# Layer norm's two halves on ScalarE and VectorE, the second token tile's transposes three steps earlier, and the first w1 pieces split by GpSimd

## The chip, the cores and the metric

The kernel runs on one core of one Trainium2 chip. The metric is the device time of one execution in microseconds; a verdict rests on the median of several runs.

## What is computed

Two transformer layers over 512 tokens of width 1024, in float32. Layer 0 mixes tokens with a top-k attention over a compressed key, layer 1 with a differential attention; each is followed by a squared-ReLU MLP of width 4096. What bears on the change is the frame around them:

```python
for i in range(DEPTH):
    sh_t, sc_t, g_t, sh_c, sc_c, g_c = jnp.split(mod[i], 6, axis=-1)
    h = x * (1.0 + sc_t) + sh_t
    y = mixer_i(h)
    x = _layer_norm(DN_ALPHA * x + (1.0 + g_t) * y, ln_g[i, 0], ln_b[i, 0])
    h = x * (1.0 + sc_c) + sh_c
    y = jnp.square(jax.nn.relu(h @ w1)) @ w2
    x = _layer_norm(DN_ALPHA * x + (1.0 + g_c) * y, ln_g[i, 1], ln_b[i, 1])
```

So there are four layer norms: after each mixer, after the first MLP, and at the end of the kernel.

## The kernel before

The 512 tokens are four tiles of 128 rows (i = 0 to 3). The residual `R[i]` is two pages of 128x512 floats, the halves h = 0 and 1 of the 1024 features. Every matrix product is made of three fp32r matmuls: an operand is split into a high part and a low part (`split_sb`, L131: ScalarE casts the high part, VectorE or GpSimd subtracts it), and `mm3` (L156 to L160) multiplies low by high, high by high and high by low. A weight piece is loaded and split by `wpiece` (L138 to L154): ScalarE casts 128x1024 at L148, then L153 subtracts, in one instruction on VectorE or in two of 128x512 on GpSimd; without an engine named, the pieces take turns.

The end of a mixer is `mixer_out.rest` (from L1005). For each tile and half the output projection takes 24 matmuls (eight steps k of three, L984 to L986) into one PSUM bank, called (i, h) here. `add_scaled` (L485) multiplies the bank by the gain on VectorE (L488) and adds the product to `R[i][h]` on VectorE or GpSimd (L489). Then `finish` (L537) makes the layer norm: `bn_stats` of both halves (L494), `bn_aggr` (L496), 1/sqrt(variance + eps) in two GpSimd instructions (L386, L387), and both halves normalised by VectorE (L549). `to_hT` (L518) transposes the tile on TensorE, four 128x128 blocks a half into a bank of the tag `t` (L522; these eight matmuls are called T0 to T3 by tile), applies scale and shift of the next stage, either on ScalarE in four 128x128 pieces (L533) or on VectorE in two 128x512 instructions (L527, L529), and splits the result into `hth` and `htl` (L133, L134). There are two banks `t` and three buffers `bm` for the result of scale and shift.

Behind it the MLP begins. Its first four w1 pieces (n = 0 to 3) run over tokens 0 to 255 first, 24 matmuls of 128x256 each, so that they need only tiles 0 and 1; then the same pieces run over tokens 256 to 511, for which tiles 2 and 3 must be in `hth` and `htl`.

A tile scheduler sets the order of the instructions on each engine. It goes by its own estimate of times and by constraints that the source gives: the table handed to `mixer_out` says behind which transposes a step of the projection may be issued, `{(2, 1, 3): "lead", (3, 1, 0): 0, (3, 1, 3): 1}` meaning that step k = 0 of (3, 1) comes behind T0 and k = 3 of (3, 1) behind T1. Once built, an engine runs its list strictly in that order, and DMAs are issued by SP in its order.

Of the kernel before, what the change touches and what calls it, by code (L numbers as in the profile page):

```python
# [15 lines left out]
ALU = mybir.AluOpType  # L16
# [51 lines left out]
def hybrid_kernel(  # L68
# [36 lines left out]
    def small(shape, tag, bufs=4):  # L105
        return tp.tile(shape, F32, tag=tag, name=nm(tag), bufs=bufs)
# [277 lines left out]
    def rstd_of(var, scale, tag):  # L384
        r = small([P, 1], tag)
        nc.gpsimd.tensor_scalar(out=r, in0=var, scalar1=scale, scalar2=EPS, op0=ALU.mult, op1=ALU.add)  # L386
        nc.gpsimd.tensor_tensor(out=r, in0=r, in1=mhalf, op=ALU.pow)  # L387
        return r
# [82 lines left out]
    def gain(l, v, tag="pg"):  # L471

        g1 = small([P, 8], "g1", 2)
        nc.vector.tensor_scalar(out=g1, in0=modc[:, l, v, :], scalar1=1.0, scalar2=None, op0=ALU.add)
        g = [temp(tag) if tag in TB else page(tag=tag) for _ in range(2)]
        for h in range(2):
            o = bank("t")
            for m in range(4):
                nc.tensor.matmul(o[:, P * m : P * (m + 1)], g1[:, 4 * h + m : 4 * h + m + 1].to_broadcast([P, P]), ident,
                                 start=True, stop=True)  # L480
            nc.scalar.copy(g[h], o)
        return g


    def add_scaled(R, h, o, g, eng):  # L485
# [2 lines left out]
        nc.vector.tensor_tensor(out=t, in0=o, in1=g[h], op=ALU.mult)  # L488
        eng.tensor_tensor(out=R[h], in0=R[h], in1=t, op=ALU.add)  # L489

    def ln_stats(R):
        st = small([P, 2, 6], "bnst")
        for h in range(2):
            nc.vector.bn_stats(out=st[:, h, :], in_=R[h])  # L494
        mv = small([P, 2], "bnmv")
        nc.vector.bn_aggr(out=mv, in_=st)  # L496
        return mv, rstd_of(mv[:, 1:2], 1.0, "lnr")

    def ln_pages(l, s, tag):
        res = []  # L500
# [17 lines left out]
    def to_hT(R, i, A, B, hT):  # L518
        for h in range(2):
            tb = bank("t")  # L520
            for m in range(4):
                last = nc.tensor.transpose(tb[:, P * m : P * (m + 1)], R[h][:, P * m : P * (m + 1)], ident)  # L522
            v = temp("bm")
            vv = v.rearrange("p (m t) -> p m t", m=4)
            if (h+i)%2:
                c = slice(4 * h, 4 * h + 4)
                nc.vector.tensor_tensor(out=vv, in0=tb.rearrange("p (m t) -> p m t", m=4),  # L527
                                        in1=A[:, c].unsqueeze(2).to_broadcast([P, 4, P]), op=ALU.mult)
                nc.vector.tensor_tensor(out=vv, in0=vv, in1=B[:, c].unsqueeze(2).to_broadcast([P, 4, P]), op=ALU.add)  # L529
            else:  # L530
                for m in range(4):
                    k = 4 * h + m
                    nc.scalar.activation(v[:, P * m : P * (m + 1)], tb[:, P * m : P * (m + 1)], AF.Identity,  # L533
                                         scale=A[:, k : k + 1], bias=B[:, k : k + 1])
            split_sb(vv, hT[0][:, 4 * h : 4 * h + 4, P * i : P * (i + 1)], hT[1][:, 4 * h : 4 * h + 4, P * i : P * (i + 1)],
                     nc.vector)
        return last.ins  # L537

    def finish(R, i, ln, coef, hT):
        mv, r = ln_stats(R)  # L540
        if coef is None:
            for h in range(2):
                nc.vector.scalar_tensor_tensor(out=R[h], in0=R[h], scalar=mv[:, 0:1], in1=ln[0][h], op0=ALU.subtract,
                                               op1=ALU.mult)
                nc.vector.scalar_tensor_tensor(out=R[h], in0=R[h], scalar=r, in1=ln[1][h], op0=ALU.mult, op1=ALU.add)
                nc.sync.dma_start(out[P * i : P * (i + 1), 512 * h : 512 * (h + 1)], R[h])
            return
        for h in range(2):
            nc.vector.tensor_scalar(out=R[h], in0=R[h], scalar1=mv[:, 0:1], scalar2=r, op0=ALU.subtract, op1=ALU.mult)  # L549
        later.append((R, ln))  # L550
        return to_hT(R, i, coef[0], coef[1], hT)

# [15 lines left out]
    def out_proj(w, act, nk, lead, tags, engs):  # L568
# [20 lines left out]
        R, g, fin = yield  # L589
        for i, o in zip(lead, os):  # L590
            add_scaled(R[i], 0, o, g, nc.gpsimd)
        for i in range(NT):
            if i not in lead:
                o = wide_bank()
                for k in range(nk):
                    step(pcs, o, i, k)
                add_scaled(R[i], 0, o, g, nc.gpsimd)
        pcs = pieces(1)
        if fin is None:
            os = [wide_bank() for i in range(NT)]  # L600
            for k in range(nk):
                for i in range(NT):
                    step(pcs, os[i], i, k)
            for i in range(NT):
                add_scaled(R[i], 1, os[i], g, nc.gpsimd)
        else:
            for i in range(NT):
                o = wide_bank()
                for k in range(nk):
                    step(pcs, o, i, k)  # L610
                add_scaled(R[i], 1, o, g, nc.vector)
                if i > 0:
                    fin(i - 1)
            fin(NT - 1)
# [347 lines left out]
    def mixer_out(w, src, R, ln_idx, prepare, mT, ring, order, late=lambda: None):  # L962
# [46 lines left out]
        def rest():  # L1009
            late()  # L1010
            mT.extend(new_hT())
            tags = {(1, 1): "l", (2, 0): "l", (2, 1): "o", (3, 0): "d", (3, 1): "d"}
            for i in range(NT):
                for h in range(2):
                    if (i, h) not in acc:
                        acc[i, h] = bank(tags[i, h])
                        for k in range(8):
                            m = [marks[order[t]] for t in order if t <= (i, h, k)]
                            with tc.issue_after(m[-1]) if m else nullcontext():
                                step(i, h, k)  # L1020
                    add_scaled(R[i], h, acc[i, h], gc[0], nc.vector if i in (0,) or (i, h) == (3, 1) else nc.gpsimd)
                marks[i] = finish(R[i], i, ln_idx, gc[1], mT)

        return weights(), first, rest
# [20 lines left out]
            for h in range(2):  # L1045
                nc.scalar.activation(R[i][h], R[i][h], AF.Copy, scale=ALPHA)

    attend(range(8), make_a, work, pv_a, done_a, mixer_out(a_w_o[0], oA, R, (0, 0), before_out_a, mT, 6, {(2, 1, 3): "lead", (3, 1, 0): 0, (3, 1, 3): 1}, scale_residual), 4, topk, 2, 2, side)


    def mlp(l, hT, ln_idx, coef_fn, side):
# [4 lines left out]
        for q in range(4):  # L1056
# [22 lines left out]
            ws, os = [], []  # L1079
            for n in range(8):  # L1080
                c0 = 1024 * q + P * n
                w = wpiece((8, P), w1[:, :, c0 : c0 + P])
                o = wide_bank()
                if q == 0 and n < 4:
                    ws.append(w)
# [8 lines left out]
                    act(o)  # L1094
            if q == 0:
                for _ in range(3 if l == 0 else 0):
                    next(side, None)
                gc = gain(l, 5, "vo")
            fin = None
            if q == 3:  # L1100
# [107 lines left out]
    def done_b(p):  # L1208
# [15 lines left out]
        for i in range(NT):  # L1224
# [4 lines left out]

    mT = []  # L1230
    attend(range(8), make_b, None, pv_b, done_b,
           mixer_out(b_w_o[0], oB, R, (1, 0), lambda: (gain(1, 2, "hk"), next_coeffs(1, 0, 1, 3, 4)), mT, 6, {(2, 1, 3): "lead", (3, 1, 0): 0, (3, 1, 3): 1}), 3,
           tick=affine_later())
    mlp(1, mT, (1, 1), None, iter(()))

# [29 lines left out]
```

## Time and profile before

| | us |
|---|---|
| median of three runs | 1312.59 (1311.4 to 1314.78) |
| the profiled execution's own time | 1311.5 |
| its span | 1309.7 |
| TensorE busy in the span | 1267.0 (97%) |
| VectorE, ScalarE, GpSimd busy | 741.5, 504.2, 570.5 |

The span is what the profiler sees of the execution; 1.8 us of its own time lie around it. Times inside the span count from its start. "Granted clock" is the share of TensorE's full clock that it was given in a stretch: 1.00 is 2.4 GHz, 0.50 is 1.2 GHz.

### The profile page before, as it was taken

The numbers are of one execution on the slowest core, as the hardware profiler recorded it, in microseconds if no ns is written. First come the engines' busy times: TensorE is split into PE (matmuls) and PEld (weight loads), VectorE is DVE, ScalarE is ACT, GpSimd is POOL, SyncE is SP. The second block draws the span as 40 slices with busy tenths as digits, with TensorE's granted clock in tenths as the row PEclk, the third lists the DMA queues.
The fourth block names the chain that finished last, engine by engine and source line by source line (L and its number), as shares of the span: only waits on it lengthen the run. The fifth ranks groups of instructions, "written<-read, shape, count | busy, mean of one in ns | idle before, by whom it ended". The sixth has DMA issues, their size and how long they took to land.

```text
span 1309.7 us, 17697 instructions
## 1 busy us (share of the span) xinstructions
PE 1267.0 (97%) x6354; PEld 1013.4 (77%) x6354; DVE 741.5 (57%) x1553; ACT 504.2 (38%) x965; POOL 570.5 (44%) x469
## 2 busy tenths in 40 slices
PE   6999999998999999999999999999899999999997
PEld 4775566677988878878788898877798888888885
DVE  2487859968642774764646376684853342332437
ACT  2554247824432422412315555682453232231320
POOL 1614348604486235234134873451539623424403
PEclk9999999999999999999999999999999999999998
DMA  9727577543623684684422633440144333333311
GB/s 308 215 82 223 168 199 200 150 137 104 187 93 108 201 256 118 210 277 141 141 81 65 177 82 104 129 129 1 49 145 125 100 97 97 97 97 97 97 49 64
DMA packets 169135, 176.79 MB, mean 135 GB/s; under 512 B 13564, under 2 KB 121432, under 8 KB 169048
## 3 DMA queue, kind: packets, MB, share of 16 engines
q1 hardware_dynamic: 169048, 175.67, 45.1%
q8 instruction: 50, 0.82, 0.3%
q14 instruction: 37, 0.30, 0.1%
HBM read 160.93 MB, written 2.12 MB: 124 GB/s over the span
## 4 chain that ended last, share of the span: by engine, by line
PE 72%; DVE 6%; POOL 2%; issue 1%; ACT 1%; DMA 0%; POOLq 0%; DVEq 0%
PE psd L158 5%; PE psd L160 5%; PE psd L159 5%; PE psl L158 3%; PE psl L159 3%; PE psl L160 3%; PE psl L578 3%; PE psl L580 3%; PE psl L579 3%; PE pso L580 3%; PE pso L578 3%; PE psd L580 3%; PE pso L579 3%; PE pso L158 3%; PE psd L578 3%; PE pso L159 3%
## 5 line engine op out<-in xcount | busy, mean ns | idle before, releaser
L153 POOL TENSOR_TENSOR wl<-raw,wh 128x512 fp32r<-128x512 f32 (+1 forms) x226 | 302.2, 1361 | 505.5 <-ACT wh L148 477.7
L148 ACT CAST wh<-raw 128x1024 fp32r<-128x1024 f32 x181 | 189.8, 1050 | 425.0 <-PE psd L580 77.9
L153 DVE TENSOR_TENSOR wl<-raw,wh 128x1024 fp32r<-128x1024 f32 x68 | 91.1, 1339 | 150.0 <-ACT wh L148 150.0
L158 PE MATMUL psd<-htl,wh 128*128 128x512 f32 (+1 forms) x400 | 157.0, 392 | 3.2 <-DVE htl L134 2.7
L159 PE MATMUL psd<-hth,wh 128*128 128x512 f32 (+1 forms) x400 | 155.1, 388 | 0.0
L160 PE MATMUL psd<-hth,wl 128*128 128x512 f32 (+1 forms) x400 | 154.7, 387 | 0.0
L489 POOL TENSOR_TENSOR rq<-rq,pt 128x512 f32<-128x512 f32 x66 | 96.7, 1495 | 76.2 <-DVE pt L488 76.1
L158 PEld LDWEIGHTS psd<-htl,wh 128*128 128x128 f32 x400 | 76.6, 191 | 25.9 <-DVE htl L134 6.0
L679 ACT ACTIVATE ex<-neg,mx 128x128 f32<-128x128 f32 (+3 forms) x128 | 72.1, 564 | 50.3 <-DVE mx L673 42.5
L160 PEld LDWEIGHTS psd<-hth,wl 128*128 128x128 f32 x400 | 76.7, 192 | 16.3 <-issue 1.7
L159 PEld LDWEIGHTS psd<-hth,wh 128*128 128x128 f32 x400 | 76.7, 192 | 13.7 <-issue 0.8
L158 PE MATMUL psl<-htl,wh 128*128 128x512 f32 (+1 forms) x224 | 82.2, 367 | 4.2 <-DVE htl L134 4.2
L159 PE MATMUL psl<-hth,wh 128*128 128x512 f32 (+1 forms) x224 | 81.9, 366 | 0.0
L160 PE MATMUL psl<-hth,wl 128*128 128x512 f32 (+1 forms) x224 | 81.3, 364 | 0.0
L134 DVE TENSOR_TENSOR pg<-ex,pg 128x512 fp32r<-128x512 f32 x66 | 60.4, 917 | 27.1 <-ACT pg L133 27.1
L580 PE MATMUL psl<-wh,pg 128*128 128x512 f32 x176 | 68.9, 391 | 0.0
L578 PE MATMUL pso<-wh,pg 128*128 128x512 f32 x176 | 68.8, 391 | 0.0
L580 PE MATMUL pso<-wh,pg 128*128 128x512 f32 x176 | 68.7, 390 | 0.0
L578 PE MATMUL psl<-wh,pg 128*128 128x512 f32 x176 | 68.7, 390 | 0.0
L579 PE MATMUL pso<-wl,pg 128*128 128x512 f32 x176 | 68.7, 390 | 0.0
L579 PE MATMUL psl<-wl,pg 128*128 128x512 f32 x176 | 68.5, 389 | 0.0
L159 PE MATMUL pso<-hth,wh 128*128 128x512 f32 (+2 forms) x184 | 68.3, 371 | 0.0
(311 smaller groups left out, 2920.9 us busy)
## 6 DMA issues: line engine op xcount, KB each, us to landing
raw<-in_mlp_w_dram SPq DMA_DIRECT2D x128, 512.0 KB, 4.1
raw<-in_ada_w_dram SPq DMA_DIRECT2D x32, 512.0 KB, 4.2
hk<-in_ada_w_dram SPq DMA_DIRECT2D x48, 256.0 KB, 3.6
bm<-in_ada_w_dram SPq DMA_DIRECT2D x48, 256.0 KB, 4.9
raw<-in_b_w_in_dram SPq DMA_DIRECT2D x24, 512.0 KB, 4.0
pg<-pg SPq DMA_DIRECT2D x84, 128.0 KB, 2.4
pg<-in_ada_w_dram SPq DMA_DIRECT2D x32, 256.0 KB, 6.0
raw<-in_a_w_in_dram SPq DMA_DIRECT2D x14, 512.0 KB, 5.1
```

The costliest lines, as they stand in the source:

```text
L134: eng.tensor_tensor(out=L, in0=src, in1=f(H), op=ALU.subtract)
L148: nc.scalar.copy(Hv, r)
L153: eng.tensor_tensor(out=Lv[:, a:b], in0=r[:, a:b], in1=f(Hv[:, a:b]), op=ALU.subtract)
L158: nc.tensor.matmul(o, w[0], a[1], start=first, stop=False)
L159: nc.tensor.matmul(o, w[0], a[0], start=False, stop=False)
L160: nc.tensor.matmul(o, w[1], a[0], start=False, stop=last)
L489: eng.tensor_tensor(out=R[h], in0=R[h], in1=t, op=ALU.add)
L578: nc.tensor.matmul(o, al[1], wr[0], start=(k == 0), stop=False)
L579: nc.tensor.matmul(o, al[0], wr[1], start=False, stop=False)
L580: nc.tensor.matmul(o, al[0], wr[0], start=False, stop=(k == nk - 1))
L679: marks["a"] = nc.scalar.activation(e[:, 0:W], neg[:, 0:W], AF.Exp, bias=mx[:, 0:1], scale=-1.0, accum_out=sums[:, m : m + 1]).ins
```

## The change

The statistics of a half are taken as soon as it is summed (`half_stats`). The variance gets its eps on VectorE, and GpSimd keeps only the power. Half 0 is normalised on ScalarE, by scale and bias (the bias, minus mean times 1/std, is one more small VectorE instruction), half 1 on VectorE as before. The result of scale and shift goes to buffers of the tag `ex`, of which there are six, where it went to the three of `bm`; VectorE's share of it is now four instructions of 128x128 with two scalars where it was two of 128x512. The sums of tile 1 move from GpSimd to VectorE. In the table, T0 now stands ahead of step 5 of (3, 0) and T1 ahead of step 0 of (3, 1). The first four w1 pieces of an MLP are all split by GpSimd. The gain's broadcast is written as a transpose.

```diff
             for m in range(4):
-                nc.tensor.matmul(o[:, P * m : P * (m + 1)], g1[:, 4 * h + m : 4 * h + m + 1].to_broadcast([P, P]), ident,
-                                 start=True, stop=True)
+                nc.tensor.transpose(o[:, P * m : P * (m + 1)], g1[:, 4 * h + m : 4 * h + m + 1].to_broadcast([P, P]), ident)
...
+    halves = {}
+
+    def half_stats(R, h):
+
+        if id(R) not in halves:
+            halves[id(R)] = small([P, 2, 6], "bnst")
+        nc.vector.bn_stats(out=halves[id(R)][:, h, :], in_=R[h])
+
     def ln_stats(R):
-        st = small([P, 2, 6], "bnst")
-        for h in range(2):
-            nc.vector.bn_stats(out=st[:, h, :], in_=R[h])
         mv = small([P, 2], "bnmv")
-        nc.vector.bn_aggr(out=mv, in_=st)
-        return mv, rstd_of(mv[:, 1:2], 1.0, "lnr")
+        nc.vector.bn_aggr(out=mv, in_=halves.pop(id(R)))
+        v = small([P, 1], "bnve")
+        nc.vector.tensor_scalar(out=v, in0=mv[:, 1:2], scalar1=EPS, scalar2=None, op0=ALU.add)
+        r = small([P, 1], "lnr")
+        nc.gpsimd.tensor_tensor(out=r, in0=v, in1=mhalf, op=ALU.pow)
+        return mv, r
...
-            v = temp("bm")
+            v = temp("ex")
             vv = v.rearrange("p (m t) -> p m t", m=4)
             if (h+i)%2:
-                c = slice(4 * h, 4 * h + 4)
-                nc.vector.tensor_tensor(out=vv, in0=tb.rearrange("p (m t) -> p m t", m=4),
-                                        in1=A[:, c].unsqueeze(2).to_broadcast([P, 4, P]), op=ALU.mult)
-                nc.vector.tensor_tensor(out=vv, in0=vv, in1=B[:, c].unsqueeze(2).to_broadcast([P, 4, P]), op=ALU.add)
+                for m in range(4):
+                    k = 4 * h + m
+                    nc.vector.tensor_scalar(out=v[:, P * m : P * (m + 1)], in0=tb[:, P * m : P * (m + 1)],
+                                            scalar1=A[:, k : k + 1], scalar2=B[:, k : k + 1], op0=ALU.mult, op1=ALU.add)
...
-        for h in range(2):
-            nc.vector.tensor_scalar(out=R[h], in0=R[h], scalar1=mv[:, 0:1], scalar2=r, op0=ALU.subtract, op1=ALU.mult)
+        nm = small([P, 1], "lnm")
+        nc.vector.tensor_scalar(out=nm, in0=mv[:, 0:1], scalar1=r, scalar2=-1.0, op0=ALU.mult, op1=ALU.mult)
+        nc.scalar.activation(R[0], R[0], AF.Identity, scale=r, bias=nm)
+        nc.vector.tensor_scalar(out=R[1], in0=R[1], scalar1=mv[:, 0:1], scalar2=r, op0=ALU.subtract, op1=ALU.mult)
...
-                    add_scaled(R[i], h, acc[i, h], gc[0], nc.vector if i in (0,) or (i, h) == (3, 1) else nc.gpsimd)
+                    add_scaled(R[i], h, acc[i, h], gc[0], nc.vector if i < 2 or (i, h) == (3, 1) else nc.gpsimd)
+                    half_stats(R[i], h)
                 marks[i] = finish(R[i], i, ln_idx, gc[1], mT)
...
-{(2, 1, 3): "lead", (3, 1, 0): 0, (3, 1, 3): 1}
+{(2, 1, 3): "lead", (3, 0, 5): 0, (3, 1, 0): 1}
...
-                w = wpiece((8, P), w1[:, :, c0 : c0 + P])
+                w = wpiece((8, P), w1[:, :, c0 : c0 + P], nc.gpsimd if q == 0 and n < 4 else None)
```

How the built order moves, at the three places of the first mixer's end that count (the second mixer's end is alike). On TensorE around T0: `psd_3591` and `psd_3606` are the bank (3, 0), `psd_3619` is (3, 1), `rq_3001` and `rq_3003` are the halves of tile 0. Before:

```order
L984 MATMUL psd_3591<-pg_2738,vo_3380 128x512
L985 MATMUL psd_3591<-pg_2740,pg_3379 128x512
L986 MATMUL psd_3591<-pg_2738,pg_3379 128x512
L522 MATMUL pst_3418<-ident,rq_3001 128x128 x4
L522 MATMUL pst_3430<-ident,rq_3003 128x128 x4
L984 MATMUL psd_3619<-wh_1953,vo_3041 128x512
L985 MATMUL psd_3619<-wl_1954,pg_3040 128x512
```

Now:

```order
L992 MATMUL psd_3606<-wh_2393,vo_3174 128x512
L993 MATMUL psd_3606<-wl_2394,pg_3173 128x512
L994 MATMUL psd_3606<-wh_2393,pg_3173 128x512
L530 MATMUL pst_3421<-ident,rq_3001 128x128 x4
L530 MATMUL pst_3433<-ident,rq_3003 128x128 x4
L992 MATMUL psd_3606<-wh_2515,vo_3219 128x512
L993 MATMUL psd_3606<-wl_2516,pg_3218 128x512
```

T0 stood behind all 24 matmuls of (3, 0) and stands behind 15 of them; T1 moved from 9 matmuls into (3, 1) to its start, and T2 from 15 matmuls behind T1 to 24 behind it.

On VectorE between the first `bn_aggr` and the normalisation of tiles 0 and 1 (`bnmv_3411` is tile 0, `bnmv_3474` and `bnmv_3479` are tile 1, `bnmv_3562` and `bnmv_3572` are tile 2). Before:

```order
L496 BN_AGGR bnmv_3411<-bnst_3408 128x2
L488 TENSOR_TENSOR pt_3556<-pso_3531,hk_3020 128x512
L494 BN_STATS bnst_3559<-rq_3009 128x6
L496 BN_AGGR bnmv_3474<-bnst_3471 128x2
L549 TENSOR_SCALAR rq_3001<-rq_3001,bnmv_3411,lnr_3413 128x512
L549 TENSOR_SCALAR rq_3003<-rq_3003,bnmv_3411,lnr_3413 128x512
L494 BN_STATS bnst_3559<-rq_3011 128x6
L549 TENSOR_SCALAR rq_3005<-rq_3005,bnmv_3474,lnr_3476 128x512
L549 TENSOR_SCALAR rq_3007<-rq_3007,bnmv_3474,lnr_3476 128x512
L496 BN_AGGR bnmv_3562<-bnst_3559 128x2
L488 TENSOR_TENSOR pt_3616<-psd_3591,hk_3019 128x512
L549 TENSOR_SCALAR rq_3009<-rq_3009,bnmv_3562,lnr_3564 128x512
```

Now:

```order
L500 BN_AGGR bnmv_3411<-bnst_3405 128x2
L496 BN_STATS bnst_3541<-rq_3009 128x6
L496 BN_STATS bnst_3448<-rq_3007 128x6
L502 TENSOR_SCALAR bnve_3413<-bnmv_3411 128x1
L500 BN_AGGR bnmv_3479<-bnst_3448 128x2
L496 BN_STATS bnst_3541<-rq_3011 128x6
L502 TENSOR_SCALAR bnve_3481<-bnmv_3479 128x1
L557 TENSOR_SCALAR lnm_3417<-bnmv_3411,lnr_3415 128x1
L559 TENSOR_SCALAR rq_3003<-rq_3003,bnmv_3411,lnr_3415 128x512
L500 BN_AGGR bnmv_3572<-bnst_3541 128x2
L557 TENSOR_SCALAR lnm_3485<-bnmv_3479,lnr_3483 128x1
L559 TENSOR_SCALAR rq_3007<-rq_3007,bnmv_3479,lnr_3483 128x512
```

The last statistic of tile 2 now stands ahead of tile 0's normalisation, each tile has two more small instructions, and the 128x512 normalisation of half 0 is gone from this list.

On TensorE around T3, where the first four w1 pieces pass from tokens 0 to 255 (`psl_3780`, `psl_3802` are piece n = 3) to tokens 256 to 511 (`psd_3706` is n = 0 again). Before:

```order
L158 MATMUL psl_3780<-htl_3401,wh_3776 128x256
L522 MATMUL pst_3657<-ident,rq_3013 128x128 x4
L522 MATMUL pst_3667<-ident,rq_3015 128x128 x4
L159 MATMUL psl_3780<-hth_3400,wh_3776 128x256
L160 MATMUL psl_3780<-hth_3400,wl_3777 128x256
```

Now:

```order
L160 MATMUL psl_3802<-hth_3400,wl_3798 128x256
L530 MATMUL pst_3675<-ident,rq_3013 128x128 x4
L530 MATMUL pst_3687<-ident,rq_3015 128x128 x4
L440 MATMUL pst_4133<-pg_3345,ones 32x512
L440 MATMUL pst_4133<-pg_3346,ones 32x512
L158 MATMUL psd_3706<-htl_3401,wh_3701 128x256
L159 MATMUL psd_3706<-hth_3400,wh_3701 128x256
```

T3 had 14 matmuls of piece n = 3 and the two L440 behind it ahead of the next token half; it has only the two L440 now.

## Rows read from the trace of the kernel before

**Rows 1.** The page, busy time, share of the span and instructions of each engine.

```profile
PE 1267.0 (97%) x6354; PEld 1013.4 (77%) x6354; DVE 741.5 (57%) x1553; ACT 504.2 (38%) x965; POOL 570.5 (44%) x469
```

**Rows 2.** Waits of TensorE, whole span: line, releaser, us in total, times, longest.

```profile
PE psl L158 <- DVE htl L134: 4.2, 1, 4.2
...
PE psd L158 <- DVE htl L134: 2.7, 3, 2.3
```

**Rows 3.** Timeline of TensorE, first mixer's end: start us, us, instruction [idle before].

```profile
305.67 0.39 PE L984 MATMUL psd<-wh,vo 128*128 128x512 f32 x1
...
311.11 1.03 PE L522 MATMUL pst<-ident,rq 128*128 128x128 f32 x8
...
320.91 0.66 PE L522 MATMUL pst<-ident,rq 128*128 128x128 f32 x4 [1.53 <-ACT bm L533]
323.91 0.58 PE L158 MATMUL psd<-htl,wh 128*128 128x256 f32 x1 [2.35 <-DVE htl L134]
...
336.45 1.04 PE L522 MATMUL pst<-ident,rq 128*128 128x128 f32 x8
...
340.32 0.39 PE L158 MATMUL psd<-htl,wh 128*128 128x256 f32 x1 [0.19 <-DVE htl L134]
```

**Rows 4.** Two stretches: us; PE, PEld, DVE, ACT, POOL busy (count); granted clock; DMA, GB/s.

```profile
324.00:329.70 5.70, 5.70 (x27) 5.70 (x28) 5.70 (x9) 4.70 (x7) 2.71 (x2) 0.50 0.74 201
...
329.70:336.00 6.30, 6.30 (x54) 6.30 (x54) 3.83 (x4) 0.00 (x0) 3.06 (x3) 0.99 0.85 256
```

**Rows 5.** Timeline of VectorE, first mixer's end.

```profile
299.75 1.37 DVE L488 TENSOR_TENSOR pt<-psd,hk 128x512 f32<-128x512 f32 x2 [1.69 <-PE psd L986]
...
304.62 1.87 DVE L494 BATCH_NORM_STATS2 bnst<-rq 128x6 f32<-128x512 f32 x3
...
307.78 1.74 DVE L549 TENSOR_SCALAR rq<-rq,bnmv,lnr 128x512 f32<-128x512 f32 x2
```

**Rows 6.** Timelines of ScalarE and GpSimd, first mixer's end.

```profile
298.16 1.25 ACT L1046 ACTIVATE rq<-rq 128x512 f32<-128x512 f32 x2 [0.82 <-DMA rq<-in_x_dram]
...
311.75 1.51 ACT L533 ACTIVATE bm<-pst,nxb,nxa 128x128 f32<-128x128 f32 x4 [10.18 <-PE pst L522]
...
306.97 0.56 POOL L387 TENSOR_TENSOR lnr<-lnr,mhalf 128x1 f32<-128x1 f32 x1
```

**Rows 7.** Timeline of VectorE, second mixer's last scores: a small instruction, and 128x128 from PSUM.

```profile
895.22 0.27 DVE L1195 TENSOR_SCALAR sl<-sums,neglam,rs 128x1 f32<-128x1 f32 x1
895.41 1.12 DVE L1223 TENSOR_SCALAR bm<-pso,bss 128x128 f32<-128x128 f32 x4
```

**Rows 8.** Timeline of GpSimd: a w piece split in two, beside VectorE's 128x1024 and alone.

```profile
326.99 3.85 POOL L153 TENSOR_TENSOR wl<-raw,wh 128x512 fp32r<-128x512 f32 x2 [6.62 <-ACT wh L148]
...
346.59 2.55 POOL L153 TENSOR_TENSOR wl<-raw,wh 128x512 fp32r<-128x512 f32 x2 [13.65 <-ACT wh L148]
```

**Rows 9.** The page, DMA issues: KB each, median us to landing.

```profile
raw<-in_mlp_w_dram SPq DMA_DIRECT2D x128, 512.0 KB, 4.1
```

**Rows 10.** Timeline of TensorE at two other waits, and a stretch behind the first.

```profile
97.69 1.91 PE L398 MATMUL pso<-raw,silrep 128*32 128x512 f32 x4 [2.01 <-DMA raw<-in_ada_w_dram]
...
98.00:98.50 0.50, 0.50 (x2) 0.00 (x0) 0.36 (x1) 0.50 (x2) 0.00 (x0) 0.50 0.99 346
...
876.60 0.47 PE L646 MATMUL psl<-pg,pg 128*128 128x512 f32 x1 [1.27 <-DVE bss L1218]
```

**Rows 11.** Timelines at the second mixer's end: one of VectorE, two of TensorE.

```profile
921.10 1.37 DVE L488 TENSOR_TENSOR pt<-psd,hk 128x512 f32<-128x512 f32 x2 [1.73 <-PE psd L986]
...
945.65 0.58 PE L158 MATMUL psl<-htl,wh 128*128 128x256 f32 x1 [4.17 <-DVE htl L134]
...
961.07 0.36 PE L158 MATMUL psl<-htl,wh 128*128 128x256 f32 x1
```

**Rows 12.** The chain that ended last, in order of time, last layer norm.

```profile
1303.44 0.75 POOL lnr L386
...
1305.24 0.75 DVE rq L545
```

More of the change, by code (lines that the diff above doesn't have):

```diff
@@ L591, in out_proj @@
             add_scaled(R[i], 0, o, g, nc.gpsimd)
[L592 to L597, printed above, removed]
+            if fin is not None:
+                half_stats(R[i], 0)
+        assert len(lead) == NT
         pcs = pieces(1)
@@ L611, in out_proj @@
                 add_scaled(R[i], 1, o, g, nc.vector)
+                half_stats(R[i], 1)
                 if i > 0:
@@ L1046, in scale_residual @@
                 nc.scalar.activation(R[i][h], R[i][h], AF.Copy, scale=ALPHA)
-    attend(range(8), make_a, work, pv_a, done_a, mixer_out(a_w_o[0], oA, R, (0, 0), before_out_a, mT, 6, {(2, 1, 3): "lead", (3, 1, 0): 0, (3, 1, 3): 1}, scale_residual), 4, topk, 2, 2, side)
+    attend(range(8), make_a, work, pv_a, done_a, mixer_out(a_w_o[0], oA, R, (0, 0), before_out_a, mT, 6, {(2, 1, 3): "lead", (3, 0, 5): 0, (3, 1, 0): 1}, scale_residual), 4, topk, 2, 2, side)
     def mlp(l, hT, ln_idx, coef_fn, side):
@@ L1096, in mlp @@
                 for _ in range(3 if l == 0 else 0):
-                    next(side, None)
+                    side_step()
                 gc = gain(l, 5, "vo")
@@ L1231, in hybrid_kernel @@
     attend(range(8), make_b, None, pv_b, done_b,
-           mixer_out(b_w_o[0], oB, R, (1, 0), lambda: (gain(1, 2, "hk"), next_coeffs(1, 0, 1, 3, 4)), mT, 6, {(2, 1, 3): "lead", (3, 1, 0): 0, (3, 1, 3): 1}), 3,
+           mixer_out(b_w_o[0], oB, R, (1, 0), lambda: (gain(1, 2, "hk"), next_coeffs(1, 0, 1, 3, 4)), mT, 6, {(2, 1, 3): "lead", (3, 0, 5): 0, (3, 1, 0): 1}), 3,
            tick=affine_later())
```

## The prediction

> **What bounds the kernel now.** I read the page first: TensorE is busy for 97% of the span [rows 1], so a change off TensorE can only win where TensorE waits. The list of its waits comes next: two of its longest are for VectorE's `htl`, once for 4.2 us and three times for 2.7 us together [rows 2]. The timeline puts them at the end of the two mixers. In the first, the second half of T2 waits 1.53 us, because both `t` banks are full and ScalarE has not yet scaled T1; then the first w1 matmul waits 2.35 us, to 323.91, for the last `htl` of tile 1 [rows 3]. In the second it waits 4.17 us, to 945.65 [rows 11]. Next I read the clock. Behind the wait TensorE was granted 0.50, the 1.2 GHz level: 27 matmuls in 5.70 us, 0.21 us each; behind that, at 2.4 GHz, 54 in 6.30 us, 0.12 each [rows 4]. A fall thus costs 27 times 0.09, or 2.5 us, by the pitch, and half of 5.7, or 2.9 us, by the stretch; I take 2.7. The last thing I read is the end: the chain there runs through both GpSimd instructions of the last tile [rows 12].
>
> **The first mixer's end, walked through with the new order.** I start where VectorE starts, at 299.75 [rows 5]; TensorE is as far as before there.
>
> *T0.* VectorE's 128x512 instructions follow each other every 0.6 us (three in 1.87) [rows 5]. Before, thirteen of them and two `bn_aggr` lie ahead of the first normalisation at 307.78. Now there are sixteen (two residual adds of tile 1 that were GpSimd's, and tile 2's last statistic), 1.8 us more, and two added variance instructions. Small ones take 0.27 us [rows 7], about 0.15 apart. So the bias `lnm` starts at 307.78 + 1.8 + 0.3 = 309.9; GpSimd's power, 0.56 [rows 6], is done by then. The bias is ready at 310.2. ScalarE's normalisation of 128x512 is not in the trace: two scalings of that shape take 1.25 us, 0.62 each, and four 128x128 pieces with scale and bias take 1.51 [rows 6]. The shape decides, so I take 0.65; the other end is 1.51. Tile 0 is ready at 310.95. TensorE asks for it after 15 matmuls of (3, 0): 24 take 311.11 - 305.67 = 5.44 us [rows 3], 0.227 each, so at 309.07. **T0 gets a new wait of 1.9 us** that was not there before.
>
> *To the first w1 matmul.* T0 takes 0.8, nine matmuls 2.0, T1 0.8, 24 matmuls 5.4, T2 0.8: 320.8. I add 0.2 for T1's second half, whose bank VectorE clears at 314.2: its four instructions of 128x128 from PSUM take 1.12 [rows 7], behind tile 2's normalisation. That makes **321.05**. What must be ready by then is tile 1's `htl`. ScalarE scales T1 from 315.0 to 316.5, casts two w1 pieces and then tile 1's two `hth`, to 319.6; VectorE's last subtraction ends at 320.35. So T2 covers it and the wait of 2.35 us goes; T2's own 1.53 us goes too, since 24 matmuls and not 15 lie ahead of it. If T0 came at once, `htl` would be next and the w1 matmul would stand at 320.4. GpSimd splits the first piece from 317.6 on, in two of 1.28 us when alone [rows 8], so the pieces come every 2.6 us, while TensorE takes 24 times 0.12, 2.9 us, for each: hidden, with 0.7 us to spare at the second.
>
> *To the second token half.* Four pieces take 11.5 us at full clock: T3 starts at 332.55. Before, the first matmul of the second half followed T3's start by 340.32 - 336.45 = 3.87 us [rows 3], through ScalarE's four pieces, its cast and VectorE's subtraction, and 14 matmuls lay in that time. ScalarE's order is the same now, so 3.87 stays, but the matmuls lie ahead of T3, so **a second new wait of about 1.8 us** opens. The second half starts at 336.4: **3.9 us saved**, of which about 2.7 is the clock.
>
> *What T3 may be late by.* ScalarE casts the fifth and sixth pieces ahead of tile 3's half 0. The sixth's load waits until GpSimd has split the third piece, at 325.8; 4.1 us of landing [rows 9], 1.05 of cast and 0.65 bring tile 3 to 331.6, and a landing of 5 to 6 us to 333.5. T3 is then 0 to 0.9 us late; I take 0.5.
>
> **The second mixer's end** has the same order on each engine that matters; it begins 921.10 - 299.75 = 621.35 us later [rows 5, 11]. First w1 matmul 942.4, T3 953.9, second half 957.8 where it was 961.07 [rows 11]: 3.3 us, and 0.2 for two gain transposes that came later before. **3.5 us**, less the same 0.5.
>
> **The end of the kernel.** One GpSimd instruction of 0.75 us leaves the last chain and a VectorE one of about 0.2 enters it. But the power runs beside the two VectorE instructions ahead of the output, which end at about 1305.05, and the output now starts at 1305.24 [rows 12]. **0.2 us.**
>
> **At nothing.** At the first MLP's end TensorE does not wait; T3 there keeps 15 matmuls, 3.4 us, ahead of the tile that needs it. That cover hides the longer ScalarE part; gone, it would cost the 1.8 us above. The gain's eight transposes keep their number. The side loads that SP issues earlier go to free buffers; the last layer norm's pages are needed 300 us later.
>
> **Sum.** 3.9 + 3.5 + 0.2 - 1.0 = 6.6 us. The profiled execution took 1311.5 us and would take 1304.9; the median is 1.1 above it, so against the median 1312.59 the forecast is **1306.0 us**.
>
> **The rivals.**
>
> *The clock falls in one or two of the new waits.* For it: a single wait of 2.01 us behind light work was followed by 0.50 [rows 10]. Against it: one of 1.27 was not, and behind it the stretch of the trace shows full clock [rows 10]; mine are 1.9 amid dense matmuls, and 1.2 and 0.6 with narrow work between. There are four such places, two per mixer. One fall gives 1308.7, two give 1311.4. Chance 0.37, of which 0.21 is one.
>
> *The clock falls in all four, the other side.* Four falls cost 10.8 us and take back more than the 6.6: 1316.8, slower. From three on the gain is gone. It needs all places to be like the 2.01 us wait; T0's lies behind matmuls, which speaks against it. Chance 0.07.
>
> *GpSimd paces the first pieces.* Beside VectorE's two-input work one piece took 3.85 us [rows 8], more than TensorE's 2.9. Then the fourth piece is 1.4 us late and T3 another 0.5, in both mixers: 1306.0 + 3.8 = 1309.8. Against it: VectorE has few instructions between 317 and 330. Chance 0.07. The Trainium skill (GPSIMD Engine Reference, Engine selection) says that two-input elementwise work belongs on VectorE, GpSimd being about twice as slow, which speaks against handing it these pieces; the trace agrees on the speed: 2.55 us when alone [rows 8].
>
> *ScalarE is the bound.* If its normalisation takes 1.51 instead of 0.65, T0's scaling is 1.7 us later, the halves on ScalarE do not do what they should, and each mixer keeps 1.3 us less: 1308.6. Chance 0.04.
>
> **How the numbers follow.** The forecast has 0.45; its own range is 1303.5 to 1308.0, from T3 not late and T0 half a microsecond earlier, to T3 late by 0.9 and T0 half a microsecond later. The four rivals have 0.55. The range 1303.3 to 1312.5 reaches over two falls and leaves out all four, and the tails. A measurement of this kernel can tell about 0.3%, 3.9 us, from no change: 1308.65. Below lie nearly all of the forecast (0.42), half of one fall (0.10) and parts of the others (0.03): faster 0.55. Slower needs 1316.5 or more: 0.06. Same: 0.39.
>
> **What would show it.** In the changed profile: a TensorE wait of 1.6 to 2.3 us ahead of T0 for ScalarE's `rq`, at both mixers; none ahead of T2; the first w1 matmul near 321 and 942.4; no wait for `htl` there; one of 1 to 2 us between T3 and the second token half; first pieces at 0.12 us a matmul. Granted clock 0.50 behind T0 or T3 would show the first rival; a w1 matmul waiting for GpSimd's `wl` the third. The forecast is wrong if the first w1 matmul still stands near 323.9, or if T0's wait exceeds 3 us, for then VectorE's list ahead of tile 0 is longer than walked here.

## The result, and the profile after

| | before | changed |
|---|---|---|
| median (us) | 1312.56 (1311.4 to 1314.78, 6 runs) | 1304.07 (1301.63 to 1308.78, 6 runs) |
| the profiled execution, its span | 1311.5, 1309.7 | 1301.63, 1299.9 |
| TensorE busy, instructions | 1267.0, 6354 | 1257.2, 6322 |

The changed kernel takes 0.9936 of the time before (95% interval 0.992 to 0.9952; the intervals behind the ratios below are of the same kind). The forecast was 1306.0, so the number came out; most of its terms did not. The page answers to [rows 1]:

```profile
PE 1257.2 (97%) x6322; PEld 1006.1 (77%) x6322; DVE 739.4 (57%) x1593; ACT 512.7 (39%) x977; POOL 571.9 (44%) x457
```

TensorE is still busy for 97%, with 32 instructions fewer. Its waits at the mixers' ends, in the list of waits [rows 2]:

```profile
PE pst L530 <- ACT rq L558: 4.0, 2, 2.2
...
PE psd L158 <- DVE htl L134: 1.8, 2, 1.0
PE psl L158 <- DVE htl L134: 1.6, 2, 1.0
...
PE pst L479 <- DVE ex L536: 1.0, 1, 1.0
PE pst L440 <- DVE ex L536: 1.0, 1, 1.0
```

The long ones of 2.3 and 4.2 us are gone, and each mixer has four shorter ones. The timeline of TensorE puts them in place, first mixer and then second [rows 3, 11]:

```profile
307.41 1.97 PE L530 MATMUL pst<-ident,rq 128*128 128x128 f32 x8 [2.21 <-ACT rq L558]
...
320.40 0.39 PE L158 MATMUL psd<-htl,wh 128*128 128x256 f32 x1 [1.05 <-DVE htl L134]
...
332.02 1.04 PE L530 MATMUL pst<-ident,rq 128*128 128x128 f32 x8
334.08 1.05 PE L440 MATMUL pst<-pg,ones 128*32 128x512 f32 x4 [1.02 <-DVE ex L536]
335.89 0.38 PE L158 MATMUL psd<-htl,wh 128*128 128x256 f32 x1 [0.76 <-DVE htl L134]
...
926.44 1.09 PE L530 MATMUL pst<-ident,rq 128*128 128x128 f32 x8 [1.78 <-ACT rq L558]
...
937.88 0.39 PE L158 MATMUL psl<-htl,wh 128*128 128x256 f32 x1 [1.05 <-DVE htl L134]
...
949.49 1.04 PE L530 MATMUL pst<-ident,rq 128*128 128x128 f32 x8
951.54 1.23 PE L479 MATMUL pst<-ident,g 128*128 128x128 f32 x8 [1.02 <-DVE ex L536]
953.36 0.39 PE L158 MATMUL psl<-htl,wh 128*128 128x256 f32 x1 [0.58 <-DVE htl L134]
```

In sum 5.04 and 4.43 us of waiting, where the kernel before had 4.26 (0.19, 1.53, 2.35, 0.19) and 4.35 (0.18, 4.17). **The waits changed places and did not get less.** What follows them did: two windows of TensorE, the granted clock being the third number from the end [rows 4]:

```profile
307.00:310.50 3.50, 3.09 (x12) 2.80 (x13) 2.53 (x10) 3.06 (x7) 0.57 (x2) 0.55 0.00 0
...
320.50:332.00 11.50, 11.50 (x96) 11.50 (x97) 9.74 (x14) 5.11 (x6) 10.58 (x8) 1.00 0.66 190
```

By windows of half a microsecond, 0.50 was granted for 3.4 us behind T0 in the first mixer, and nowhere in the second. The kernel before had 6.8 us at 0.50 in each, behind its long wait.

To see where the time went, I cut each span at landmarks: VectorE's first product of the residual at each mixer's end (L488 before, L487 after), the first w1 matmul of the second token half, TensorE's last matmul and VectorE's last instruction (starts, us).

| | start to mixer 1 | mixer 1 | to mixer 2 | mixer 2 | to last matmul | end |
|---|---|---|---|---|---|---|
| before | 299.75 | 40.57 | 580.78 | 39.97 | 338.96 | 5.21 |
| changed | 295.72 | 40.17 | 578.84 | 38.63 | 337.81 | 4.24 |
| changed, again (e1) | 294.86 | 40.20 | 578.06 | 38.63 | 337.81 | 4.24 |
| gain and eps alone (e6) | 300.09 | 39.88 | 579.46 | 40.32 | 337.80 | 4.25 |
| halves on VectorE (e9) | 300.33 | 37.46 | 578.51 | 37.46 | 337.80 | 4.24 |
| mended order (e8) | 296.00 | 36.63 | 579.51 | 36.76 | 337.80 | 4.24 |

The first column is mostly chance: near 97 us, behind a wait of 2 us for a DMA [rows 10], the profiles of before, e6 and e9 have 6.8 us or more at 0.50, e8 3.4, the changed kernel and e1 none, though they wait there for 1.97 and 2.04 us; nor has e4 (below), which keeps the order of before and starts mixer 1 at 295.99. From there on the changed kernel is 5.8 us shorter than before, and 1.7 of that lie in the mixers, of which the first is shorter by only 0.40 us.

### The profile page after: what moved, and what is told of

It reads as the page before. It is cut to its first block, busy times and chain, and to the rows that moved or that the text cites. A ratio compares the mean times of both kernels' runs of the same rounds, so it can differ in the third digit from the quotient of the medians.

```text
span 1299.9 us, 17649 instructions
## 1 busy us (share of the span) xinstructions
PE 1257.2 (97%) x6322; PEld 1006.1 (77%) x6322; DVE 739.4 (57%) x1593; ACT 512.7 (39%) x977; POOL 571.9 (44%) x457
## 4 chain that ended last, share of the span: by engine, by line
PE 88%; DVE 5%; DMA 4%; ACT 1%; issue 1%; SPq 1%; POOL 0%; DVEq 0%; ACTq 0%; POOLq 0%
PE psd L158 7%; PE psd L160 7%; PE psd L159 7%; PE psl L158 3%; PE psl L160 3%; PE psl L159 3%; PE pso L590 3%; PE psl L588 3%; PE psl L590 3%; PE pso L588 3%; PE pso L589 3%; PE psl L589 3%; PE pso L158 3%; PE pso L160 3%; PE pso L159 3%; PE psd L590 3%
## 5 line engine op out<-in xcount | busy, mean ns | idle before, releaser
L153 POOL TENSOR_TENSOR wl<-raw,wh 128x512 fp32r<-128x512 f32 (+1 forms) x234 | 315.2, 1372 | 484.8 <-ACT wh L148 471.0
L488 POOL TENSOR_TENSOR rq<-rq,pt 128x512 f32<-128x512 f32 x62 | 92.3, 1519 | 98.9 <-DVE pt L487 97.0
L160 PE MATMUL pso<-hth,wl 128*128 128x512 f32 (+2 forms) x184 | 68.2, 371 | 0.0
```

The source lines that it names most:

```text
L153: eng.tensor_tensor(out=Lv[:, a:b], in0=r[:, a:b], in1=f(Hv[:, a:b]), op=ALU.subtract)
L160: nc.tensor.matmul(o, w[1], a[0], start=False, stop=last)
```

## The experiments

**e1, the changed kernel again.**

> The changed kernel itself a second time. The stage that counts is from VectorE's first product of the residual (L487, 128x512 x2) to the first w1 matmul over tokens 256 to 511: 40.57 and 39.97 us in the kernel before (first and second mixer, a stretch at granted clock 0.50 in each), 40.17 and 38.63 in the changed kernel (one such stretch, in the first). Theory W (the waits were shortened): both mixers again have the sum of waits of the first trace, and the time stands 6 to 9 us below the kernel before whatever the clock does. Theory C (the waits only changed places, 4.4 to 5.0 us per mixer before and after, and the gain is that TensorE's clock falls less): the waits come back to 0.1 us (T0 2.2 and 1.8, first w1 matmul 1.05 twice, behind T3 1.0 and 0.6 to 0.8), and a mixer with a stretch at 0.50 takes about 40.2, one without about 38.5. The 4.0 us that the changed kernel was ahead at the start of the first mixer's end come from the 0.50 stretch that only the kernel before had at 98 to 104 us; if that was chance, this run may have one there or not.

Median 1302.21 (1300.05 to 1309.28), ratio 0.9938 (0.9915 to 0.9961). All waits came back within 0.03 us. Theory C (the waits only changed places, and the clock falls less behind them) holds for the mixers, as the table shows; it says nothing yet of the other stages. Behind T0's wait of 2.21 us 0.50 was granted from 307 on again; behind the 1.77 us in the second mixer it was not.

**e5 and e4, two small parts of the change, each alone on the kernel before; e6, both; e7, all the rest.** e5 is the gain's edit, e4 this:

```diff
-        return mv, rstd_of(mv[:, 1:2], 1.0, "lnr")
+        v = small([P, 1], "bnve")
+        nc.vector.tensor_scalar(out=v, in0=mv[:, 1:2], scalar1=EPS, scalar2=None, op0=ALU.add)
+        r = small([P, 1], "lnr")
+        nc.gpsimd.tensor_tensor(out=r, in0=v, in1=mhalf, op=ALU.pow)
+        return mv, r
```

> The kernel before with one part of the change alone: the gain's broadcast written as a transpose. The prediction had it at nothing, eight instructions per gain as before: then the time is that of the kernel before, 1311.6. My account now: a 128x128 product with the identity in float32 is two records on TensorE (16 in 1.95 us for one gain at 379.30 in the kernel before), a transpose is one (8 in 1.03 us at 382.79 in the changed kernel), 0.92 us less for each of four gains, and TensorE is busy for 97%: 2.9 to 3.7 us, 1308 to 1308.7.

> The kernel before with one part of the change alone: eps added by VectorE, GpSimd left with the power. My account now: at the end of the kernel VectorE takes 5.61 us a tile (1295.36 to 1300.97) where TensorE delivers one each 5.44, so VectorE is 0.9 us behind TensorE's last matmul at the last tile; without its wait of 0.44 us for GpSimd it takes 5.2 a tile, is paced by TensorE, and the time from the start of the last matmul to the start of the last VectorE instruction falls from 5.21 to 4.24 us: 1.0 us less, 1311.5 in all. The prediction's account was 0.2 us, from the last chain alone: 5.0 us and 1312.4. At the mixers' ends GpSimd's first instruction (0.2 to 0.7 us) leaves tile 0's chain, at most 0.5 us, and the clock falls as before.

> The kernel before with the two parts that do not belong to the order at the mixers' ends: the gain as a transpose, and eps added by VectorE. If these two are the whole gain, this kernel takes what the changed one does, 1302 to 1304. If the rest of the change (halves, order, tile 1's sums, GpSimd's pieces) earns what the prediction gave it, 3.9 and 3.5 us, this one stands at 1306.5 to 1308. If the rest earns only a clock that falls less, 2 to 3 us, it stands at 1305 to 1306.5, and its profile has 0.50 stretches of 6.8 us at the mixers' ends.

> The changed kernel with those two parts undone: gain as a product with the identity, eps and power on GpSimd. The prediction's mixers alone give 7.4 us less 1.0, 1305.2. If the mixers' ends gained nothing but the clock, 1308 to 1310; if not even that, 1311 to 1312. T0's wait should be near that of the changed kernel, 1.8 to 2.5 us, and the end of the kernel has the 5.2 us of the kernel before between the starts of the last matmul and the last VectorE instruction, not 4.24.

| | median (us) | ratio to before | mean granted clock |
|---|---|---|---|
| before (73 runs beside these kernels) | 1311.97 | | 0.990 |
| e5, gain | 1306.65 | 0.9968 (0.9951 to 0.9985) | 0.990 |
| e4, eps | 1308.01 | 0.9973 (0.9958 to 0.9987) | 0.992 |
| e6, both | 1306.94 | 0.9959 (0.9942 to 0.9976) | 0.990 |
| e7, the rest | 1319.74 | 1.005 (1.003 to 1.0071) | 0.990 |
| changed (12 runs with e1) | 1302.8 | 0.9936, 0.9938 | 0.994 |

*The gain is worth about 4 us* at an equal mean clock: 4.2 by the ratio, with an interval from 2.0 to 6.4. The profile before had said so. TensorE's groups by line, shapes apart (count, then busy us and mean ns), first before, then changed:

```profile
L522 PE MATMUL pst<-ident,rq 128*128 128x128 f32 x96 | 13.3, 275 | 2.0 <-ACT bm L533 1.7 <-DVE bm L527 0.2
L479 PE MATMUL pst<-ident,g 128*128 128x128 f32 x64 | 8.5, 278 | 0.0
```

```profile
L530 PE MATMUL pst<-ident,rq 128*128 128x128 f32 x96 | 13.4, 286 | 4.0 <-ACT rq L558 4.0
L479 PE MATMUL pst<-ident,g 128*128 128x128 f32 x32 | 5.4, 304 | 1.0 <-DVE ex L536 1.0
```

The 96 transposes of the layer norms (three norms, four tiles, eight each) are 96 records; the 32 products of the four gains are 64. A float32 product with the identity runs as two, a transpose of the same shape as one. At 379.30 one gain took 1.95 us in 16 records, in the changed kernel 1.03 in eight: 0.92 us each, 3.7 for four, on an engine that is busy for 97%. The Trainium skill (TensorE: Matmul & The Clock Gate, Terms) calls its transpose mode four times faster for FP32. The trace agrees on which of the two is faster, but here it is 1.9 times faster, not four.

*The eps part*: in e4 too the end takes 4.24 us, as expected, and in e7, which has GpSimd's two instructions back, 5.20; so the prediction's 0.2 falls. What e4 gained beyond that 1.0 us (3.5 in all by the ratio) may be the clock (0.992 against 0.990); it wasn't tried apart.

*Both together*: 1306.94 lies in the case in which the rest keeps its 3.9 and 3.5 us, close to the one in which it earns only the clock. The rows decide: e6's mixers take 80.20 us, the changed kernel's 78.80, so the rest earned 1.4 us there and not six. TensorE waits 4.19 us in e6's second mixer, as before, with 6.8 us at 0.50 behind it; the first mixer has 3.4. The changed kernel's two mixers have 3.4 us at 0.50 in all, so the difference in the clock alone covers the 1.4.

*The rest alone is slower than before*, which no theory had. Its list of waits:

```profile
PE pst L527 <- ACT rq L555: 7.4, 4, 2.5
...
PE psd L1138 <- DVE htl L134: 1.6, 1, 1.6
```

With GpSimd's two-step root, T0 waits 2.47 and 2.41, T3 another 1.28 and 1.23 for ScalarE's half, and the first MLP's end, which had no wait in any other kernel shown here, gets 0.47 and 1.62, with a 3.4 us stretch at 0.50 behind it. So it seems that the mixers' edits need the short root (eps added by VectorE, GpSimd left with the power). It isn't shown apart: e7 has the old gain as well.

**e2, T0 later, and e10, the old table, both on the changed kernel.** The table's last two entries become `(3, 1, 0): 0, (3, 1, 2): 1` and `(3, 1, 0): 0, (3, 1, 3): 1`.

> The changed kernel with T0 behind all of (3, 0) and T1 behind two steps of (3, 1). If the new wait ahead of T0 (2.2 and 1.8 us) is lost time, as the prediction had it: nine matmuls of 0.227, 2.0 us, cover it, the wait falls below 0.4 us, T1 and with it tile 1's htl come 2 us earlier relative to T0's readiness, and the first w1 matmul comes 1.5 to 2 us earlier in both mixers: 3 to 4 us faster than the changed kernel. If instead tile 1's htl sets the time, because ScalarE casts w1 pieces ahead of it and GpSimd's splits slow VectorE, the wait only moves to the first w1 matmul (1.05 becomes 2 to 3 us) and the time is the same within 1 us.

> The changed kernel with the table of before: T0 behind all of (3, 0), T1 behind three steps of (3, 1). The run with T0 later and T1 behind two steps lost the wait ahead of T0 but gained one of 3.7 us ahead of the first w1 matmul. If the wait depends on how late T1 comes, this one has 3 to 4 us there in both mixers, the clock falls behind it as in the kernel before, and the time is 1305 to 1307. If the wait was made by T1's second half (1.0 us for a bank), which this order leaves more room for, the first w1 matmul waits under 3 us and the time is 1302 to 1304.

e2: 1306.26, ratio 0.9954 (0.9936 to 0.9971). e10: 1304.63, 0.9932 (0.9907 to 0.9958). TensorE's timeline in e2, second mixer:

```profile
933.65 0.66 PE L530 MATMUL pst<-ident,rq 128*128 128x128 f32 x4 [1.02 <-DVE ex L536]
...
943.09 0.39 PE L158 MATMUL psl<-htl,wh 128*128 128x256 f32 x1 [3.78 <-DVE htl L134]
```

T0's wait fell to 0.19 us and came back at the first w1 matmul; in e10 it is 3.13 and 3.21 there, with mixers of 38.86 and 38.62 us. So T0's wait was not lost time: tile 1's `htl` set the end behind it. The transposes three steps forward are worth nothing that these times resolve, and the rows speak against them: with 3.4 us at 0.50 in each, e10's first mixer takes 38.86 us and the changed kernel's 40.17.

**e3, tile 1 ahead of the w1 casts, on the changed kernel.** The ScalarE casts that the block makes are queued behind the two `hth` casts of tile 1; what it makes on other engines is not:

```diff
+                    if q == 0 and n < 2:
+                        es.enter_context(tc.issue_after(mk["hth", 1, 0]))
+                        es.enter_context(tc.issue_after(mk["hth", 1, 1]))
                     w = wpiece((8, P), w1[:, :, c0 : c0 + P], nc.gpsimd if q == 0 and n < 4 else None)
```

> The changed kernel with ScalarE's casts of the first two w1 pieces behind both casts of tile 1 (hth). If VectorE's last two subtractions of tile 1 took 3.36 us for two because GpSimd was splitting a w1 piece beside them (1.3 alone), they now end before GpSimd has a piece and take 1.3 to 1.5; htl is ready 3 us earlier, and the wait of 1.05 us before the first w1 matmul goes: 1.0 us per mixer, 2 in all. If the two subtractions take long for another reason (they wait for ScalarE, or the operands), they still take over 2.5 us and the wait stays above 0.5.

1305.37, ratio 0.9969 (0.9952 to 0.9986). The last two subtractions of tile 1, first in the changed kernel (first mixer; 3.36 us in the second too) with GpSimd's pieces beside them, then in e3 (second mixer; 1.27 us in the first), where GpSimd starts its first piece 0.9 us after the first of them (timelines of VectorE, GpSimd and VectorE):

```profile
316.99 3.36 DVE L134 TENSOR_TENSOR htl<-ex,hth 128x512 fp32r<-128x512 f32 x2 [1.05 <-ACT hth L133]
```

```profile
315.57 12.30 POOL L153 TENSOR_TENSOR wl<-raw,wh 128x512 fp32r<-128x512 f32 x8 [0.96 <-ACT wh L148]
```

```profile
934.75 1.28 DVE L134 TENSOR_TENSOR htl<-ex,hth 128x512 fp32r<-128x512 f32 x2
```

Beside GpSimd's split they take 3.36 us, nearly clear of it 1.28, and the wait before the first w1 matmul is gone. The Trainium skill (SBUF — State Buffer, SBUF: two separate sides) has VectorE and GpSimd share a port pair that one instruction holds to its end; the trace agrees, 1.68 us for a subtraction being near GpSimd's 1.54 for a half piece. But the time isn't better. Behind T3, in e3 (TensorE, then VectorE):

```profile
953.84 1.09 PE L481 MATMUL pst<-ident,g 128*128 128x128 f32 x8 [3.24 <-DVE ex L538]
```

```profile
951.28 1.23 DVE L155 TENSOR_TENSOR wl<-raw,wh 128x1024 fp32r<-128x1024 f32 x1 [3.16 <-ACT wh L150]
952.42 1.36 DVE L538 TENSOR_SCALAR ex<-pst,nxa,nxb 128x128 f32<-128x128 f32 x4
```

T3's scaling now stands behind a later w1 piece on VectorE, and so behind its cast, for which ScalarE itself waited 2.53 us for a DMA.

**e9, both halves on VectorE, and e11, the first four pieces in turns, on the changed kernel.** e9 puts back the two `tensor_scalar` of L549; e11 drops the `nc.gpsimd` of L1091.

> The changed kernel with both halves normalised by VectorE again. In the changed kernel ScalarE's half of tile 0 runs from 306.54 to 307.36 and TensorE waits for it; VectorE takes 0.45 us for a half when GpSimd is not beside it (two between 306.43 and 307.6), so both halves of tile 0 would be ready at about the same time. If sharing the halves earns nothing, T0's wait stays at 1.6 to 2.3 us and the time within 1.5 us of the changed kernel's 1302 to 1304, at an equal clock. If sharing is what made tile 0 early, the wait ahead of T0 grows by 0.5 us or more, tile 1 and 2 come 1 us later, and the time is 1305 or more.

> The changed kernel with the first four w1 pieces split in turns by GpSimd and VectorE, as before. If giving all four to GpSimd earns something, VectorE's work for tiles 2 and 3 now comes later, T3's halves with it, and the wait between T3 and the second token half grows from 1.6 to 1.8 us to 3 or more, in both mixers. If it earns nothing, the wait of 1.05 us before the first w1 matmul is the same (GpSimd still has the first piece), the one behind T3 is the same within 0.5 us, and the time stays within 1 us.

e9: 1301.95, ratio 0.9914 (0.9894 to 0.9933). T0 waits 1.69 and 1.26 us, half a microsecond *less* than with shared halves, and T3 finds 15 matmuls behind it again. TensorE, second mixer:

```profile
927.49 1.11 PE L530 MATMUL pst<-ident,rq 128*128 128x128 f32 x8 [1.26 <-DVE rq L557]
...
938.97 0.39 PE L158 MATMUL psl<-htl,wh 128*128 128x256 f32 x1 [1.08 <-DVE htl L134]
...
953.76 0.38 PE L158 MATMUL psl<-htl,wh 128*128 128x256 f32 x1 [0.29 <-DVE htl L134]
```

Both mixers take 37.46 us, 1.17 less than the changed kernel's second one; none of these three has a stretch at 0.50. **Sharing the halves, the change's main part, costs 1.2 us per mixer with this table.** About 0.5 of it is there by the first w1 matmul; the other 0.7 lies behind it, where the scheduler, by itself, put T3 back among matmuls. The medians don't resolve the 1.2 us (the intervals overlap); the rows do. e11: 1306.66, 0.9953 (0.9937 to 0.9969), mixers of 40.94 and 39.47. VectorE there:

```profile
934.61 1.47 DVE L153 TENSOR_TENSOR wl<-raw,wh 128x1024 fp32r<-128x1024 f32 x1 [0.53 <-ACT wh L148]
936.01 3.44 DVE L134 TENSOR_TENSOR htl<-ex,hth 128x512 fp32r<-128x512 f32 x2
```

The second piece's split stands ahead of tile 1's `htl`, and the w1 matmul waits 2.0 us, not 1.05. So GpSimd's four pieces earn 0.8 us per mixer by the rows (the intervals overlap here too), at another place than expected: behind T3 the waits are the same within 0.15 us.

**e8, the orders mended together, on the changed kernel; e12, the same with both halves on VectorE.** The table is `(3, 1, 0): 0, (3, 1, 4): 1`, and each piece is queued behind what it got in the way of:

```diff
+                    first = {0: "hth 1", 1: "hth 1", 3: "pow 3", 4: "norm 3", 5: "hth 3"}.get(n, "") if q == 0 else ""
+                    for ins in mk.get(first, ()):
+                        es.enter_context(tc.issue_after(ins))
...
+                    with tc.issue_after(mk["tr"]) if n == 3 else nullcontext():
+                        denseT(o, w, hT, ((0, 256),))
```

> The changed kernel with the order of the mixers' ends mended where the runs showed the waits: T0 behind all of (3, 0), T1 behind four steps of (3, 1), ScalarE's first two w1 casts behind tile 1's hth, GpSimd's power of tile 3 ahead of its fourth w1 piece, T3 ahead of the fourth piece's matmuls, and the fifth and sixth pieces behind tile 3's own work on ScalarE and VectorE. If the waits of 4.4 to 5.0 us per mixer are made by these orders, what is left is under 1.5 us per mixer: the stage from VectorE's first product to the second token half falls from 38.6 to 34.8 to 36 us without a 0.50 stretch, and the time to 1295 to 1298. If they are made by the sum of work on ScalarE and VectorE between T0 and the second half, the waits show up again in a third place and the time stays at 1301 or above.

> The mended order of e8 with both halves normalised by VectorE. With the table of the changed kernel the shared halves cost 1.2 us per mixer (38.63 against 37.46 us from VectorE's first product to the second token half) and 0.7 us at the first MLP's end (347.97 against 347.30 between the second half and T0 there). If ScalarE's half costs this wherever it stands, the mended order also gets shorter: stages of 35.5 to 36.5 us, 347.3 at the first MLP, and 1295 to 1296.5. If in the mended order VectorE is the tighter engine (two of its instructions more ahead of tile 2 and of tile 1's last htl), the stages grow by 0.5 us or more over 36.63 and 36.76, and only the first MLP's 0.7 us is gained: 1297 to 1299.

e8: 1296.99 (1296.6 to 1297.34, 4 runs), ratio 0.9884 (0.9862 to 0.9907), faster than both kernels: the interval lies below the changed kernel's in e1 (0.9915 to 0.9961), at a mean granted clock of 0.993. Mixers of 36.63 and 36.76 us, a little above the 34.8 to 36 expected, with 1.7 and 1.2 us of waiting left; in the second:

```profile
933.03 0.38 PE L160 MATMUL psl<-htl,wh 128*128 128x256 f32 x1 [0.79 <-ACT wh L150]
933.98 0.39 PE L160 MATMUL psl<-htl,wh 128*128 128x256 f32 x1 [0.45 <-ACT wh L150]
```

So most of the waiting was made by the order, not by the sum of the work. e12: 1300.82, 0.9909 (0.988 to 0.9938), above both cases named for it and not resolved from e8 by its interval; mixers of 37.37 and 37.11 us, longer as in the second case. The 0.7 us at the first MLP's end that the expectation counts are no gain: T0 comes earlier there (347.31 us), but the whole stretch to the second mixer takes 578.48 us in e12 and 578.06 in e1, both without 0.50. Its T3, second mixer (TensorE, then VectorE):

```profile
946.86 0.66 PE L533 MATMUL pst<-ident,rq 128*128 128x128 f32 x4 [0.40 <-DVE rq L563]
...
948.35 0.63 PE L533 MATMUL pst<-ident,rq 128*128 128x128 f32 x4 [0.84 <-DVE rq L563]
```

```profile
945.29 2.92 DVE L563 TENSOR_SCALAR rq<-rq,bnmv,lnr 128x512 f32<-128x512 f32 x2 [2.93 <-POOL lnr L506]
```

Here the two halves of tile 3 take 2.92 us on VectorE beside GpSimd's split, and T3 waits 1.2. In this order sharing earns 0.74 us in the first mixer (in the second, 0.35, e8 has 3.4 us at 0.50 and e12 none); in the changed kernel's it costs 1.2. What it is worth depends on what stands beside it.

## Why the prediction was right, and where it was wrong

*T0 gets a new wait of 1.9 us*: right, 2.21 and 1.78. ScalarE's 128x512 normalisation took 0.82 us, the mean of twelve, nearer to the 0.65 taken than to the other end, 1.51, at which ScalarE would have been the bound (the fourth rival). Two sums of the walk come out up to 0.1 us too high (310.2 + 0.65 is 310.85, 320.8 + 0.2 is 321.0), which changes nothing.

*The wait of 2.35 us goes, the first w1 matmul comes at 321.05*: wrong. It came at 320.40, but the mixer's end also began 4.03 us earlier, for the most part by the chance near 97 us. Counted from VectorE's first product it came after 24.68 and 23.15 us, where the walk has 21.30 and the kernel before 24.16 and 24.55. So in the first mixer the prediction's own sign of being wrong, a first w1 matmul that still stands near 323.9, is met. This is the step "VectorE's last subtraction ends at 320.35". It took 0.6 us for each subtraction, the pitch of VectorE alone, though the same text had GpSimd split the first piece from 317.6 on. e3 shows the difference, 2.1 us for two. A wait of 1.05 us stayed. Most of the rest of the delay is T0, 0.5 us late in both mixers, and in the first the clock (below).

*A second new wait of 1.8 us*: right, 1.78 and 1.60, and T3 to the second half took 3.87 us in both mixers, as predicted. *T3 late by 0.5*: not at all. *GpSimd's pieces hidden*: right for TensorE, which never waited for `wl` (the third rival); GpSimd took 1.54 us a half piece, and VectorE paid. *Nothing at the first MLP's end*: right, no wait; in e7, with the two-step root, there are two.

*3.9 and 3.5 us saved*: 0.40 and 1.34 by the table. Of the 2.7 us that were the clock's share in the first, T0's own wait gave a part back: 0.50 for 3.4 us. That is the first rival, one fall, in the changed kernel and again in e1. It cost less than the 2.7 us named for it: from T0 to T1 the first mixer took 4.56 us, the second 3.01, and e11's first mixer, with the same wait and no fall, 3.01 too. The full clock that the prediction saw behind the wait of 1.27 us is in the trace (1.00 from 876 to 884 us), not in [rows 10].

*The end, 0.2 us*: mis-sized, 0.97. The step counted the last tile's chain alone. Before, VectorE took 5.61 us a tile and TensorE 5.44, so VectorE was late when the last tile came:

```profile
1295.36 0.69 DVE L488 TENSOR_TENSOR pt<-pso,vo 128x512 f32<-128x512 f32 x1
...
1300.97 0.69 DVE L488 TENSOR_TENSOR pt<-pso,vo 128x512 f32<-128x512 f32 x1
```

Now it waits for TensorE, and half of the 0.97 us is that (timeline of VectorE, changed):

```profile
1291.59 0.69 DVE L487 TENSOR_TENSOR pt<-pso,vo 128x512 f32<-128x512 f32 x1 [0.21 <-PE pso L590]
...
1295.41 1.41 DVE L553 SCALAR_TENSOR_TENSOR rq<-rq,lnr,vo 128x512 f32<-128x512 f32 x2
```

*"The gain's eight transposes keep their number"*: the step that failed worst. It counted instructions in the source; the trace counts records, sixteen before and eight now. It was put at nothing; alone it is worth about 4 us (e5), as much as the largest term of the sum.

**So the total was right by luck, by two errors against each other**: 7.4 us from the mixers' ends, less 1.0 for T3, that gave 1.7 in the profile, and 0.2 us from two small edits that gave about 5 (e6; 3.1 to 7.6 by its interval). How much the rest of the change adds over e6 is less sure: about 3 us by the ratios, whose intervals overlap, and 1.4 in the rows of the mixers. Over all runs the changed kernel has a mean granted clock of 0.994, before and e6 have 0.990, and a run of before is 0.85 us longer for each 0.001 less, by a line through 73 runs. So the clock carries about 3 us, and at an equal clock the mixers' new order earns about nothing. That is an estimate from a trend over runs, not shown by an experiment; the rows of e6, e9 and e10 point the same way. Why the changed kernel's clock falls less often stays open.

## What to carry to other kernels

Count an edit on the busiest engine in records of the trace, not in lines of source: a group's count beside that of a like group (64 for 32 products, 96 for 96 transposes) shows what an instruction costs. A wait that goes is gained only if the next thing asked for is ready: find what that is and what its engine has ahead of it, and price VectorE beside GpSimd by rows in which both run. When waits wander from place to place, mend all the orders at once; one alone (e2, e3) gained no time here, all together took 5.4 us off the two mixers' 78.8. And compare a landmark with its distance from the stage's start, not with the span's: a chance 4 us earlier hid here that the first w1 matmul came later than before.

## What the runs showed of the hardware that was not expected

- A float32 128x128 product with the identity is two TensorE records, 16 in 1.95 us, a transpose one, eight in 1.03.
- VectorE's two-input 128x512 subtraction takes 0.64 us alone and 1.68 beside GpSimd's subtraction (1.54 each), and its one-input normalisation of two halves 2.92 us beside GpSimd's split (e12) and 0.99 in e9 at 310.92, where GpSimd has only its small power.
- The same wait is followed by 0.50 or not: 2.21 us ahead of T0 in three profiles with it (changed, e1, e3), in e11 without; 2.47 us in e7 without. Behind the DMA wait of 2.0 us near 97 us it came in before and e6, not in the changed kernel and e1. A wait's length alone did not decide it here.
